# A hybrid decoder step: output projection and gate on token chunks of 448, 448 and 160, operands kept as whole rows

## The chip, the core and the metric

The kernel runs on one core of a Trainium2 chip. A core has a matrix engine (TensorE, "PE" in the profile, with its weight loads as "PEld"), a vector engine (DVE), a scalar engine (ACT), a general engine (POOL), a sync engine (SP) that here only issues transfers, and 16 DMA engines that serve all queues. Matmuls write to PSUM, in banks of 512 float32 columns; everything else lies in SBUF, 128 partitions wide. The metric is the device time of the whole program in microseconds, the median of several runs. Before the change it is 1441.19 us (3 runs, 1440.43 to 1441.89).

## The reference

One layer of a decoder for 1024 prompt tokens and 32 sample tokens (8 sequences of 4), 1056 tokens in all, width 1024. Cut to what the change touches, it ends so:

```python
y_a = o.reshape(B, T, V_W) @ w_proj_a                      # gated delta branch
y_b = (y_pool * silu(gp)) @ w_proj_b                       # pooling branch
m = sigmoid(ga) * y_a + sigmoid(gb) * y_b
x = x + m @ w_out                                          # output projection
x = x + sigmoid(rmsnorm(x, norm_ple) @ w_ple_gate) * (p_i @ w_ple_proj)   # per-layer gate
y = rmsnorm(x, final_norm)
```

What stands ahead of it (input projections, convolution, gated delta recurrence, pooling) is computed by the same program and is not changed but for one small edit named below.

## The kernel before

Everything is kept transposed: features on the partitions (8 tiles of 128), tokens along the free dimension. The 1056 tokens are cut into three chunks of 352 (`CW`, `NCH`). A dense product takes one weight tile (128 output features, all 1024 input features) and one chunk. For precision both operands are split into a high and a low part in a float32 form that the array takes in one pass (`F32R`), and `chunk` (L317) runs 8 times three matmuls: high weight by high data, high weight by low data, low weight by high data. So a product is 24 matmuls of 128x128 weights by 352 moving columns, each with a weight load of its own. Matmuls on plain float32 operands (the recurrence, the norms) appear in the trace as two records each.

The last part of the program, from L1554 on, has six passes. In the first three the output projection runs over the eight weight tiles for chunk 0, then chunk 1, then chunk 2; `ev_o` adds the residual from an addend that is loaded a step ahead into one of three buffers (`addend`), and ACT squares the result for the norm. When a pass is over, `norm_ple` is started: sums of squares by matmuls with one moving column, a Newton iteration on DVE (`rstd`, L407), a diagonal matrix `dg` whose product with ones spreads the factor over the partitions, and then per tile a scaling, a high part on ACT, a low part on DVE or POOL. The second three passes are the gate's product on chunk 0, 1, 2 (`ev_p`: tanh on ACT, two operations on DVE, square on ACT, sum on DVE), each followed by `norm_out`, which scales and stores the chunk. The very last tile is worked in two halves. Behind the last matmul stands the tail: that tile, the norm of the last chunk, eight scalings and eight stores.

The order of the work on each engine is written by a recording layer (`Weave`): generators such as `norm_ple` are advanced between matmuls whenever a planner's clock says that their inputs are due. The planner books a matmul of a product at 13 ns plus its columns over 2.4. The engines then run their own queues in order and wait on semaphores. The weights of the output projection are split once and stay (`resident`), loaded two tiles ahead during the first pass; those of the gate come in during the third pass. PSUM has four banks for the products (`psd`) here and two for the norms (`pse`).

Operands are tiles of 128 x 352, one for each feature tile and chunk (`set_tiles`, L301): `h` (normed input, later the pooled branch), `o` (delta branch), `m` (merged branch), and `g` (normed x for the gate) in the buffers of `m`.

Of the kernel before, what the change touches and what calls it, by code (L numbers as in the profile page):

```python
# [18 lines left out]
P = 128  # L19
D = 1024  # L20
KT = D // P
# [4 lines left out]
T = TP + TS  # L26
CW = 352
NCH = T // CW
H = 8
NU = TP // P  # L30
PH = 15
# [203 lines left out]
def decoder_step(ctx, tc, A, O):  # L235
    nc = tc.nc
    wv = Weave()
# [8 lines left out]
    def mm(o, l, r, ns, start=True, stop=True):  # L246
        PE.matmul(o, l, r, start=start, stop=stop)  # L247
        wv.pe(ns)
# [50 lines left out]
        eng.tensor_tensor(out=lo, in0=src, in1=hi.bitcast(F32), op=ALU.subtract)  # L299

    def set_tiles(p, name):  # L301
        mk = lambda s: [[p.tile([P, CW], F32R, name=f"{name}{s}{k}_{n}", tag=f"{s}{k}_{n}") for n in range(NCH)]
                        for k in range(KT)]
        return mk("h"), mk("l")

    def drained(g, ps, ring):

# [94 lines left out]
            if step:  # L402
                yield step

    RB = CW // 4

    def rstd(sqs, bank, mk, key=None, keys=()):  # L407


        ms, rs, tm = (mk([P, 4], nm)[0:RB] for nm in ("ms", "rs", "tm"))  # L410
        for j, parts in enumerate([sqs] if key else [[q] for q in sqs]):
            if j:
                yield keys
            pr = bank()[0:RB, 0:4]
            for j in range(4):
                for i, q in enumerate(parts):
                    mm(pr[:, j:j + 1], q[:, j * RB:(j + 1) * RB], ones[:, 0:1], 150, start=(i == 0),
                       stop=(i == len(parts) - 1))
# [8 lines left out]
        dg = mk([P, 4, RB], "dg")[0:RB]  # L427
        V.tensor_tensor(out=dg, in0=ident[0:RB, 0:RB].unsqueeze(1).broadcast_to([RB, 4, RB]),
                        in1=rs.unsqueeze(2).broadcast_to([RB, 4, RB]), op=ALU.mult)
        yield  # L430
        bc = bank()[:, 0:CW]
        mm(bc, ones[0:RB, :], dg.rearrange("p a b -> p (a b)"), 592)
        return bc


    hhi, hlo = set_tiles(sa, "h")
# [1033 lines left out]

# [36 lines left out]
    def heads_end():  # L1507
        hctx.close()
        so = octx.enter_context(pool("seto"))
        for l, t in zip((ohi, olo), set_tiles(so, "o")):  # L1510
            l.extend(t)
# [18 lines left out]
    psd = banks(ctx, "psd", PB)  # L1530


    mhi, mlo = set_tiles(sa, "m")
    with pool("ew", 2) as ew:
        for m in range(KT):
            ta = ew.tile([P, T], F32, name="ta2", tag="ta2")
# [16 lines left out]

    cq = ctx.enter_context(pool("outp", 2))  # L1554
    pse = ctx.enter_context(pool("pse", 2, space=PSUM))
    x1 = [[cq.tile([P, CW], F32, name=f"x1{k}_{n}", bufs=1) for n in range(NCH)] for k in range(KT)]
    ct = lambda nm, bufs=2: cq.tile([P, CW], F32, name=nm, tag=nm, bufs=bufs)

    def ssum(m, sqa, src, key):
        if m == 0 or m == KT - 1 and len(sqa) > 1:  # L1560
            S.activation(sqa[m > 0], src, AF.Square)
        else:
            q = ct("sq1")
# [5 lines left out]
    def rnorm(sqs, keys=()):  # L1569
        return rstd(sqs, lambda: pse.tile([P, 512], F32, name="pse", tag="pse"),  # L1570
                    lambda sh, nm: cq.tile(sh, F32, name=nm, tag=nm, bufs=1), keys=keys)

    ghi, glo = [[None] * NCH for _ in range(KT)], [[None] * NCH for _ in range(KT)]

    def norm_ple(n, sqa):
        yield [("o", 0, n, m) for m in range(KT)]
        yield
        rs = yield from rnorm(sqa)
        yield
        for k in range(KT):  # L1580
            hh = ct("hh")
            V.scalar_tensor_tensor(out=hh, in0=x1[k][n], scalar=nple[:, k:k + 1], in1=rs, op0=ALU.mult, op1=ALU.mult)
            yield
            ghi[k][n] = sa.tile([P, CW], F32R, name=f"gh{k}_{n}", tag=f"h{k}_{n}")
            glo[k][n] = sa.tile([P, CW], F32R, name=f"gl{k}_{n}", tag=f"l{k}_{n}")
            S.copy(ghi[k][n], hh)
            yield
            (G if k % 2 else V).tensor_tensor(out=glo[k][n], in0=hh, in1=ghi[k][n].bitcast(F32), op=ALU.subtract)
        wv.mark("ple", n)

    def norm_out(n, sqa):
        done = [("o", 1, n, m) for m in range(KT)]
        yield done[:-1] if len(sqa) > 1 else done
        yield
        rs = yield from rnorm(sqa, done)
        yield
        last = n == NCH - 1
        for k in range(KT):
            V.scalar_tensor_tensor(out=x1[k][n], in0=x1[k][n], scalar=nfin[:, k:k + 1], in1=rs,
                                   op0=ALU.mult, op1=ALU.mult)  # L1600
            SY.dma_start(O["yT"][k][:, ns_(n)], x1[k][n])
            if not last:
                yield

# [29 lines left out]

    adds = {}

    def addend(s):

        if s < 48:
            n, m = s % 24 // KT, s % KT  # L1640
            adds[s] = ct("xr2", 3)
            SY.dma_start(adds[s], (A["xT"] if s < 24 else pp_d)[m][:, ns_(n)])

    addend(0)
    for n in range(NCH):
        sqa = [ct("sqa")]
        for m in range(KT):
            s = n * KT + m
            weights_step(s)
            addend(s + 1)  # L1650

            def ev_o(n, c, o, xr=adds[s], m=m, sqa=sqa):
                V.scalar_tensor_tensor(out=x1[m][n], in0=o, scalar=0.5, in1=xr, op0=ALU.mult, op1=ALU.add)
                yield
                yield from ssum(m, sqa, x1[m][n], (0, n, m))
            chunk(held["w_out"][m], mhi, mlo, n, ev_o)
        wv.add(norm_ple(n, sqa))
    for n in range(NCH):
        wv.until(("ple", n), data=True)
        sqa = [ct("sqa")] + [ct("sqb")] * (n == NCH - 1)  # L1660
        for m in range(KT):
            s = 24 + n * KT + m
            weights_step(s)
            addend(s + 1)

            def ev_p(n, c, o, pq=adds[s], m=m, sqa=sqa):
                t, x = ct("tg"), x1[m][n]
                end = n == NCH - 1 and m == KT - 1
                w = CW // 2 if end else CW
                for a in range(0, CW, w):  # L1670
                    S.activation(t[:, a:a + w], o[:, a:a + w], AF.Tanh, scale=0.5)
                    if not end:
                        yield
                for a in range(0, CW, w):
                    V.scalar_tensor_tensor(out=pq[:, a:a + w], in0=t[:, a:a + w], scalar=1.0, in1=pq[:, a:a + w],
                                           op0=ALU.add, op1=ALU.mult)
                    V.tensor_tensor(out=x[:, a:a + w], in0=x[:, a:a + w], in1=pq[:, a:a + w], op=ALU.add)
                    if end:
                        S.activation(sqa[1][:, a:a + w], x[:, a:a + w], AF.Square)
                if end:  # L1680
                    wv.mark("o", 1, n, m)
                    return
                yield
                yield from ssum(m, sqa, x1[m][n], (1, n, m))
# [73 lines left out]
```

## Time and profile before

| what | value |
|---|---|
| median of 3 runs | 1441.19 us |
| the profiled execution | 1443.41 us |
| its span on the core | 1441.6 us |
| PE busy in the span | 1400.9 us (97%) |
| granted clock of TensorE, mean | 0.991 |
| the six passes | about 1233 to 1427 us of the span |
| behind the last matmul of a product | about 14.4 us |

The profile is of one execution, 2.2 us longer than the median, and its span leaves out 1.8 us around it. Shares of busy time are averages over stages. A matmul's duration in the trace (about 323 ns at 352 columns) contains its way through the array; the next one starts long before it ends, so the rate is read from starts, or from a count in a stretch without gaps.

### The profile page before, as it was taken

What the parts mean: (1) busy time and instruction counts of PE and PEld (TensorE: products, weight loads), DVE (VectorE), ACT (ScalarE), POOL (GpSimd) and SP (SyncE); (2) the same over time, 40 slices, a digit from 0 to 9 for tenths busy, and PEclk for the clock granted to TensorE, in tenths of its full rate; (3) what the DMA queues carried; (4) which work ended last, traced back from release to release, by engine and by line L of the source; (5) the groups of instructions that cost most, each with busy time, mean ns of one, the idle gap of its engine ahead of it and who ended that gap; (6) DMA issues with size and microseconds to landing.
All of it is one profiled execution on the core that took longest, in us unless ns stands there. A gap on an engine that the chain in (4) does not pass through costs nothing.

```text
span 1441.6 us, 24421 instructions
## 1 busy us (share of the span) xinstructions
PE 1400.9 (97%) x9138; PEld 1359.4 (94%) x9138; DVE 832.8 (58%) x1810; ACT 611.2 (42%) x1612; POOL 406.6 (28%) x336
## 2 busy tenths in 40 slices
PE   8899999999999999999999999999999999999996
PEld 7799999999999999999999899999889999999996
DVE  5686666665666635437457457457464244645654
ACT  5356565555454323544454454454223122324321
POOL 3444545454121222232132132032021112315100
PEclk9899999999999999999999999999999999999998
DMA  9222232223244413752234234236538434415132
GB/s 311 72 78 94 94 104 97 96 104 123 76 135 145 136 54 104 210 176 84 66 143 132 77 124 146 65 112 222 188 122 282 139 135 147 135 46 163 43 97 88
DMA packets 106235, 178.94 MB, mean 124 GB/s; under 512 B 19260, under 2 KB 78852, under 8 KB 106116
## 3 DMA queue, kind: packets, MB, share of 16 engines
q1 hardware_dynamic: 91716, 125.99, 26.7%
q10 hardware_dynamic: 14400, 51.39, 11.5%
q8 instruction: 72, 1.18, 0.3%
q14 instruction: 47, 0.39, 0.1%
HBM read 119.92 MB, written 57.41 MB: 123 GB/s over the span
## 4 chain that ended last, share of the span: by engine, by line
PE 84%; DVE 8%; DMA 4%; ACT 2%; issue 1%; SPq 1%; POOL 0%; ACTq 0%; DVEq 0%; POOLq 0%
PE psd L247 69%; PE psg L247 5%; PE psr L247 5%; PE psg L251 2%; DMA rw<-og_d 1%; PE sr L247 1%; DVE win L186 1%; DVE big L186 1%; DMA xt<-in_xT_dram 1%; PE sg L247 1%; PE pse L247 1%; DMA gt<-tb_d 1%; DMA pp_d<-ppt 1%; DVE sg L186 1%; DMA wr<-in_w_out_dram 1%
## 5 line engine op out<-in xcount | busy, mean ns | idle before, releaser
L247 PE MATMUL psd<-hh,wh 128*128 128x352 f32 x1728 | 570.1, 330 | 5.8 <-DVE gt L186 3.4
L247 PE MATMUL psd<-hh,wl 128*128 128x352 f32 x1728 | 567.2, 328 | 0.4 <-POOL wl L186 0.4
L247 PE MATMUL psd<-hl,wh 128*128 128x352 f32 x1728 | 565.9, 327 | 0.0
L186 POOL TENSOR_TENSOR wl<-wr,wh 128x1024 fp32r<-128x1024 f32 (+1 forms) x87 | 209.9, 2412 | 612.7 <-ACT wh L186 536.2
L247 PEld LDWEIGHTS psd<-hh,wh 128*128 128x128 f32 x1728 | 326.1, 189 | 9.4 <-DVE gt L186 4.3
L247 PEld LDWEIGHTS psd<-hl,wh 128*128 128x128 f32 x1728 | 326.4, 189 | 1.8 <-issue 0.3
L247 PEld LDWEIGHTS psd<-hh,wl 128*128 128x128 f32 x1728 | 326.0, 189 | 2.2 <-POOL wl L186 0.7
L186 DVE SCALAR_TENSOR_TENSOR acc<-xr,cw,acc 128x352 f32<-128x352 f32 x144 | 108.5, 772 | 37.3 <-ACT acc L186 35.9
L186 ACT CAST wh<-wr 128x1024 fp32r<-128x1024 f32 (+1 forms) x88 | 90.6, 1030 | 40.2 <-PE psd L247 26.7
L186 POOL TENSOR_TENSOR acc<-acc,f 128x352 f32<-128x352 f32 (+1 forms) x72 | 73.6, 1028 | 120.7 <-DVE acc L186 89.1
L186 DVE SCALAR_TENSOR_TENSOR f<-f,acc 128x352 f32<-128x352 f32 (+1 forms) x72 | 68.8, 956 | 48.2 <-ACT f L186 48.2
L186 ACT ACTIVATE gt<-psd 128x352 f32<-128x352 f32 x69 | 32.3, 468 | 113.4 <-PE psd L247 88.4
L186 DVE SCALAR_TENSOR_TENSOR gt<-gt,psd 128x352 f32<-128x352 f32 x48 | 24.8, 516 | 67.0 <-ACT gt L186 30.2
L247 PE MATMUL psd<-oh,wh 128*128 128x352 f32 x192 | 62.0, 323 | 0.7 <-DVE gt L186 0.7
L247 PE MATMUL psd<-oh,wl 128*128 128x352 f32 x192 | 61.6, 321 | 0.0
L247 PE MATMUL psd<-ol,wh 128*128 128x352 f32 x192 | 61.6, 321 | 0.0
L186 ACT COPY xr<-psd 128x352 f32<-128x352 f32 (+1 forms) x96 | 33.7, 377 | 61.1 <-PE psd L247 61.1
L186 ACT ACTIVATE f<-acc 128x352 f32<-128x352 f32 (+1 forms) x72 | 36.1, 502 | 53.0 <-POOL acc L186 41.3
L186 ACT ACTIVATE junk<-psg 128x128 f32<-128x128 f32 x128 | 36.2, 283 | 41.4 <-PE psg L251 39.7
L247 PE MATMUL psd<-mh,rl 128*128 128x352 f32 x144 | 46.5, 323 | 1.1 <-POOL rl L186 1.1
L247 PE MATMUL psd<-gh,rh 128*128 128x352 f32 x144 | 46.7, 325 | 0.0
L247 PE MATMUL psd<-mh,rh 128*128 128x352 f32 x144 | 46.5, 323 | 0.0
(289 smaller groups left out, 2521.1 us busy)
## 6 DMA issues: line engine op xcount, KB each, us to landing
wr<-in_w_in_dram ACTq DMA_DIRECT2D x64, 512.0 KB, 3.6
kq_d<-f SPq DMA_DIRECT2D x16, 512.0 KB, 2.6
F<-kq_d SPq DMA_DIRECT2D x16, 512.0 KB, 4.9
xt<-in_xT_dram SPq DMA_DIRECT2D x6, 704.0 KB, 7.4
pp_d<-ppt SPq DMA_DIRECT2D x24, 176.0 KB, 6.0
yh_d<-ysh SPq DMA_DIRECT2D x24, 176.0 KB, 2.0
yl_d<-ysl SPq DMA_DIRECT2D x24, 176.0 KB, 2.6
tb_d<-gt SPq DMA_DIRECT2D x24, 176.0 KB, 3.7
```

The costliest lines, as they stand in the source:

```text
L186: return f(*a, **k)
L247: PE.matmul(o, l, r, start=start, stop=stop)
L251: PE.transpose(o, i, idn)
```

## The change

The two products of the last part take chunks of 448, 448 and 160 tokens (`LAST`) in place of three of 352. The output projection goes over them in the order first, short, second; the gate in the order first, second, short, so that the short chunk is the last. The operand tiles `h`, `o` and `m` become whole rows of 1056 tokens that are cut into views (`cut`, `thirds`), and the normed x for the gate is written over `m` in place. `rstd` takes its width from the sums of squares. While the norm of the last chunk is computed, six matmuls without use (`keep`) run on TensorE. The loops over passes and tiles become one list of steps. Apart from that, in `both` (two pairs of weight tiles between the gates and the pooled branch's projection) the second weight's low part is computed by DVE, not by POOL.

```diff
+LAST = tuple(slice(a, b) for a, b in ((0, 448), (448, 896), (896, T)))
+LW = 448
...
     def set_tiles(p, name):
-        mk = lambda s: [[p.tile([P, CW], F32R, name=f"{name}{s}{k}_{n}", tag=f"{s}{k}_{n}") for n in range(NCH)]
-                        for k in range(KT)]
+        mk = lambda s: [p.tile([P, T], F32R, name=f"{name}{s}{k}", tag=f"{s}{k}") for k in range(KT)]
         return mk("h"), mk("l")
+
+    cut = lambda tiles, cols: [[t[:, c] for c in cols] for t in tiles]
+    thirds = lambda tiles: cut(tiles, [ns_(n) for n in range(NCH)])
...
-    def rstd(sqs, bank, mk, key=None, keys=()):
+    def rstd(sqs, bank, mk, key=None, keys=(), keep=0):
+        W = sqs[0].shape[1]
+        RB = W // 4
...
+        if keep:
+            idle = bank()
+            for _ in range(keep):
+                mm(idle[:, 0:P], ident, ident, 222)
...
                 if n == NCH - 1 and raws:
-                    wv.run(split_w())
+                    wv.run(split_w(G if w is ws[0] else V))
...
-    ghi, glo = [[None] * NCH for _ in range(KT)], [[None] * NCH for _ in range(KT)]
+    ghi, glo = mhi, mlo
...
-        rs = yield from rnorm(sqa, done)
-        yield
         last = n == NCH - 1
+        rs = yield from rnorm(sqa, done, 6 if last else 0)
+        yield
...
+    steps = [(j, n, m) for j, chunks in enumerate(((0, 2, 1), (0, 1, 2))) for n in chunks for m in range(KT)]
...
+        if j:
+            chunk(held["w_ple_gate"][m], ghi, glo, n, ev_p, cols=LAST[n])
+        else:
+            chunk(held["w_out"][m], mhi, mlo, n, ev_o, cols=LAST[n])
             if m == KT - 1:
-                wv.add(norm_out(n, sqa))
-            chunk(held["w_ple_gate"][m], ghi, glo, n, ev_p)
+                wv.add(norm_ple(n, sqa))
```

On PE, the second pass of the output projection (weights `wh`, `wl`, data `mh`, `ml`), around the sums of squares of the first chunk. Before:

```order
L247 MATMUL psd_10977<-mh_1_10982,wh 128x352
L247 MATMUL psd_10977<-ml_1_11006,wh 128x352
L247 MATMUL psd_10977<-mh_1_10982,wl 128x352
L247 MATMUL psd_10977<-mh_1_10985,wh 128x352
L247 MATMUL psd_10977<-ml_1_11009,wh 128x352
```

And now, at the same place:

```order
L249 MATMUL psd_10914<-mh_10917,wh 128x160
L249 MATMUL psd_10914<-ml_10925,wh 128x160
L249 MATMUL psd_10914<-mh_10917,wl 128x160
L249 MATMUL psd_10914<-mh_10918,wh 128x160
L249 MATMUL psd_10914<-ml_10926,wh 128x160
L249 MATMUL pse<-cst,sqa 112x1 x4
```

The sequence of weights is the same and so is the number of matmuls; the second pass is now the one on 160 columns, and the other two have 448.

On PE at the end of the program (`sqa`, `sqb` are the squares, `cst` the constants). Before:

```order
L247 MATMUL psd_10980<-gh_2_13036,rh_12805 128x352
L247 MATMUL pse<-cst,sqa 88x1 x4
L247 MATMUL psd_10980<-gl_2_13037,rh_12805 128x352
L247 MATMUL psd_10980<-gh_2_13036,rl_12806 128x352
L247 MATMUL psd_10980<-gh_2_13057,rh_12805 128x352
L247 MATMUL psd_10980<-gl_2_13058,rh_12805 128x352
L247 MATMUL psd_10980<-gh_2_13057,rl_12806 128x352
L247 MATMUL pse<-cst,sqb 88x1 x4
L247 MATMUL pse<-dg,cst 128x352
```

And now:

```order
L249 MATMUL psd_10916<-mh_10924,rh_12686 128x160
L249 MATMUL psd_10916<-ml_10932,rh_12686 128x160
L249 MATMUL psd_10916<-mh_10924,rl_12687 128x160
L249 MATMUL pse<-cst,sqa 40x1 x4
L249 MATMUL pse<-cst,sqb 40x1 x4
L249 MATMUL pse<-cst 128x128 x6
L249 MATMUL pse<-dg,cst 128x160
```

The first sums of squares moved behind the last matmul of the products, and the six matmuls of `keep` stand ahead of the one that spreads the factor.

On DVE, in the projection of the pooled branch (`os` are small operations of the recurrence's output norm, `gt` the evacuation of a product, `F` of the recurrence). Before:

```order
L186 TENSOR_TENSOR os_t_7283<-os_r_7282 128x8
L186 SCALAR_TENSOR_TENSOR os_t_7283<-os_t_7283,os_x_7281 128x8
L186 SCALAR_TENSOR_TENSOR os_r_7282<-os_t_7283,os_r_7282 128x8
L186 SCALAR_TENSOR_TENSOR gt_5767<-gt_5767,psd_5725 128x352
L186 SCALAR_TENSOR_TENSOR F_5746<-psg_5729,gn,F_5746 128x512
```

And now:

```order
L188 TENSOR_TENSOR os_t_7251<-os_r_7250 128x8
L188 SCALAR_TENSOR_TENSOR os_t_7251<-os_t_7251,os_x_7249 128x8
L188 SCALAR_TENSOR_TENSOR os_r_7250<-os_t_7251,os_r_7250 128x8
L188 TENSOR_TENSOR wl<-wr,wh 128x1024
L188 SCALAR_TENSOR_TENSOR gt_5735<-gt_5735,psd_5693 128x352
L188 SCALAR_TENSOR_TENSOR F_5714<-psg_5697,gn,F_5714 128x512
```

A split of 1024 columns (`wl`) that POOL did before stands on DVE, ahead of an evacuation; another stands some 60 us earlier.

## Rows read from the trace of the kernel before

**Rows 1.** The page's part 1: busy time, share of the span, instructions.

```profile
PE 1400.9 (97%) x9138; PEld 1359.4 (94%) x9138; DVE 832.8 (58%) x1810; ACT 611.2 (42%) x1612; POOL 406.6 (28%) x336
```

**Rows 2.** Stretches of the six passes: length; busy of PE, PEld, DVE, ACT, POOL; clock; DMA.

```profile
1233.00:1263.60 30.60, 29.51 (x184) 29.06 (x183) 19.70 (x18) 10.83 (x15) 11.97 (x5) 1.00 0.46 142
1263.60:1427.20 163.60, 163.28 (x1030) 160.61 (x1028) 93.37 (x211) 49.28 (x95) 31.67 (x20) 1.00 0.29 87
```

**Rows 3.** The same view, matmuls of the products alone, inside one pass.

```profile
1272.00:1299.00 27.00, 27.00 (x169) 27.00 (x168) 3.68 (x7) 0.00 (x0) 1.00 0.16 46
```

**Rows 4.** Float32 matmuls, 128 weight columns, 96 moving: by form, then in time.

```profile
L247 PE MATMUL psg<-U,U 128*128 128x96 f32 x128 | 16.6, 274 | 0.9 <-DVE U L186 0.9
...
683.24 1.03 PE L247 MATMUL psg<-U,U 128*128 128x96 f32 x8
...
688.97 1.06 PE L247 MATMUL psg<-U,U 128*128 128x96 f32 x8
```

**Rows 5.** PEld, then PE in time (start, length) as a product resumes.

```profile
602.57 0.19 PEld L247 LDWEIGHTS psd<-hh,wh 128*128 128x128 f32 x1
602.68 0.19 PEld L247 LDWEIGHTS psd<-hl,wh 128*128 128x128 f32 x1
602.85 0.19 PEld L247 LDWEIGHTS psd<-hh,wl 128*128 128x128 f32 x1
...
602.60 0.41 PE L247 MATMUL psd<-hh,wh 128*128 128x352 f32 x1
602.84 0.32 PE L247 MATMUL psd<-hl,wh 128*128 128x352 f32 x1
```

**Rows 6.** PE and POOL in time, in the first pass.

```profile
1244.87 0.32 PE L247 MATMUL psd<-ml,rh 128*128 128x352 f32 x1
1246.27 0.43 PE L247 MATMUL psd<-mh,rl 128*128 128x352 f32 x1 [1.09 <-POOL rl L186]
...
1243.84 2.38 POOL L186 TENSOR_TENSOR rl<-wr,rh 128x1024 fp32r<-128x1024 f32 x1 [16.83 <-ACT rh L186]
```

**Rows 7.** Engines in time, in the projection of the pooled branch.

```profile
1067.28 2.35 POOL L186 TENSOR_TENSOR wl<-wr,wh 128x1024 fp32r<-128x1024 f32 x1
...
1067.38 2.27 DVE L186 TENSOR_TENSOR os_t<-os_r 128x8 f32<-128x8 f32 x1
...
1069.68 0.17 DVE L186 SCALAR_TENSOR_TENSOR os_t<-os_t,os_x 128x8 f32<-128x8 f32 x1
...
1069.97 0.52 DVE L186 SCALAR_TENSOR_TENSOR gt<-gt,psd 128x352 f32<-128x352 f32 x1
...
1070.54 0.54 PE L247 MATMUL psd<-hh,wh 128*128 128x352 f32 x1 [2.74 <-DVE gt L186]
```

**Rows 8.** The tail: engines in time; last, a stretch as in rows 2.

```profile
1426.86 0.32 PE L247 MATMUL psd<-gh,rl 128*128 128x352 f32 x1
...
1432.31 0.52 DVE L186 TENSOR_TENSOR dg<-cst,rs 88x352 f32<-88x352 f32 x1
1432.98 1.51 PE L247 MATMUL pse<-dg,cst 88*128 88x352 f32 x2 [2.82 <-DVE dg L186]
1434.53 4.02 DVE L186 SCALAR_TENSOR_TENSOR x<-x,vec,pse 128x352 f32<-128x352 f32 x8 [1.70 <-PE pse L247]
1435.14 3.78 SPq L231 DMA_DIRECT2D out_yT_dram<-x  x8
...
1429.00:1430.00 1.00, 0.86 (x8) 0.77 (x7) 0.00 (x0) 0.35 (x1) 0.00 (x0) 0.55 0.00 0
```

**Rows 9.** Groups by form in the six passes: DVE at two widths.

```profile
L186 DVE SCALAR_TENSOR_TENSOR xr<-tg,xr 128x352 f32<-128x352 f32 x23 | 12.1, 525 | 22.0 <-ACT tg L186 22.0
...
L186 DVE SCALAR_TENSOR_TENSOR xr<-tg,xr 128x176 f32<-128x176 f32 x2 | 0.7, 338 | 1.2 <-ACT tg L186 1.2
```

**Rows 10.** SP's queue in time, issues one behind the other.

```profile
1008.08 0.42 SPq L231 DMA_DIRECT2D hl<-yl_d  x1
1008.60 0.38 SPq L231 DMA_DIRECT2D hh<-yh_d  x1
```

More of the change, by code (lines that the diff above doesn't have):

```diff
@@ L425, in rstd @@
                 V.scalar_tensor_tensor(out=ms, in0=pr, scalar=1.0 / D, in1=ms, op0=ALU.mult, op1=ALU.add)
+        if keep:
+            idle = bank()
+            for _ in range(keep):
+                mm(idle[:, 0:P], ident, ident, 222)
         yield from rsqrt_steps(rs, ms, tm, 0 if key else 100)
-        dg = mk([P, 4, RB], "dg")[0:RB]
-        V.tensor_tensor(out=dg, in0=ident[0:RB, 0:RB].unsqueeze(1).broadcast_to([RB, 4, RB]),
+        dg = mk([P, CW if key else LW], "dg")[0:RB, 0:W]
+        V.tensor_tensor(out=dg.rearrange("p (a b) -> p a b", a=4), in0=ident[0:RB, 0:RB].unsqueeze(1).broadcast_to([RB, 4, RB]),
                         in1=rs.unsqueeze(2).broadcast_to([RB, 4, RB]), op=ALU.mult)
         yield
-        bc = bank()[:, 0:CW]
-        mm(bc, ones[0:RB, :], dg.rearrange("p a b -> p (a b)"), 592)
+        bc = bank()[:, 0:W]
+        mm(bc, ones[0:RB, :], dg, 1.68 * W)
         return bc
-    hhi, hlo = set_tiles(sa, "h")
+    hhi, hlo = map(thirds, set_tiles(sa, "h"))
     sq = kp.tile([P, 3, H * TS], F32, name="sq")
@@ L1510, in heads_end @@
         for l, t in zip((ohi, olo), set_tiles(so, "o")):
-            l.extend(t)
+            l.extend(thirds(t))
         op = octx.enter_context(pool("rwp"))
@@ L1530, in decoder_step @@
     psd = banks(ctx, "psd", PB)
-    mhi, mlo = set_tiles(sa, "m")
+    mset = set_tiles(sa, "m")
+    mhi, mlo = map(thirds, mset)
     with pool("ew", 2) as ew:
@@ L1555, in decoder_step @@
     pse = ctx.enter_context(pool("pse", 2, space=PSUM))
-    x1 = [[cq.tile([P, CW], F32, name=f"x1{k}_{n}", bufs=1) for n in range(NCH)] for k in range(KT)]
-    ct = lambda nm, bufs=2: cq.tile([P, CW], F32, name=nm, tag=nm, bufs=bufs)
+    width = [c.stop - c.start for c in LAST]
+    mhi, mlo = (cut(t, LAST) for t in mset)
+    x1 = [[cq.tile([P, w], F32, name=f"x1{k}_{n}", bufs=1) for n, w in enumerate(width)] for k in range(KT)]
+    ct = lambda nm, n, bufs=2: cq.tile([P, LW], F32, name=nm, tag=nm, bufs=bufs)[:, 0:width[n]]
     def ssum(m, sqa, src, key):
@@ L1562, in ssum @@
         else:
-            q = ct("sq1")
+            q = ct("sq1", key[1])
             S.activation(q, src, AF.Square)
@@ L1567, in ssum, with rnorm @@
         wv.mark("o", *key)
-    def rnorm(sqs, keys=()):
+    def rnorm(sqs, keys=(), keep=0):
         return rstd(sqs, lambda: pse.tile([P, 512], F32, name="pse", tag="pse"),
-                    lambda sh, nm: cq.tile(sh, F32, name=nm, tag=nm, bufs=1), keys=keys)
-    ghi, glo = [[None] * NCH for _ in range(KT)], [[None] * NCH for _ in range(KT)]
+                    lambda sh, nm: cq.tile(sh, F32, name=nm, tag=nm, bufs=1), keys=keys, keep=keep)
+    ghi, glo = mhi, mlo
     def norm_ple(n, sqa):
@@ L1580, in norm_ple @@
         for k in range(KT):
-            hh = ct("hh")
+            hh = ct("hh", n)
             V.scalar_tensor_tensor(out=hh, in0=x1[k][n], scalar=nple[:, k:k + 1], in1=rs, op0=ALU.mult, op1=ALU.mult)
             yield
-            ghi[k][n] = sa.tile([P, CW], F32R, name=f"gh{k}_{n}", tag=f"h{k}_{n}")
-            glo[k][n] = sa.tile([P, CW], F32R, name=f"gl{k}_{n}", tag=f"l{k}_{n}")
             S.copy(ghi[k][n], hh)
@@ L1594, in norm_out @@
         yield
-        rs = yield from rnorm(sqa, done)
+        last = n == NCH - 1
+        rs = yield from rnorm(sqa, done, 6 if last else 0)
         yield
-        last = n == NCH - 1
         for k in range(KT):
@@ L1600, in norm_out @@
                                    op0=ALU.mult, op1=ALU.mult)
-            SY.dma_start(O["yT"][k][:, ns_(n)], x1[k][n])
+            SY.dma_start(O["yT"][k][:, LAST[n]], x1[k][n])
             if not last:
@@ L1635, in decoder_step @@
     adds = {}
+    steps = [(j, n, m) for j, chunks in enumerate(((0, 2, 1), (0, 1, 2))) for n in chunks for m in range(KT)]
     def addend(s):
[L1639 to L1642, printed above, removed]
+        if s < len(steps):
+            j, n, m = steps[s]
+            adds[s] = ct("xr2", n, 3)
+            SY.dma_start(adds[s], (pp_d if j else A["xT"])[m][:, LAST[n]])
     addend(0)
[L1645 to L1653, printed above, removed]
-                yield
-                yield from ssum(m, sqa, x1[m][n], (0, n, m))
-            chunk(held["w_out"][m], mhi, mlo, n, ev_o)
-        wv.add(norm_ple(n, sqa))
@@ L1658, in decoder_step @@
[L1658 to L1679, printed above, removed]
-                if end:
[L1681 to L1684, printed above, removed]
@@ new lines, in decoder_step, with ev_o, ev_p @@
+    for s, (j, n, m) in enumerate(steps):
+        last = j and n == NCH - 1
+        if m == 0:
+            if j:
+                wv.until(("ple", n), data=True)
+            sqa = [ct("sqa", n)] + [ct("sqb", n)] * last
+        weights_step(s)
+        addend(s + 1)
+        def ev_o(n, c, o, xr=adds[s], m=m, sqa=sqa):
+            V.scalar_tensor_tensor(out=x1[m][n], in0=o, scalar=0.5, in1=xr, op0=ALU.mult, op1=ALU.add)
+            yield
+            yield from ssum(m, sqa, x1[m][n], (0, n, m))
+        def ev_p(n, c, o, pq=adds[s], m=m, sqa=sqa):
+            t, x, cw = ct("tg", n), x1[m][n], width[n]
+            end = n == NCH - 1 and m == KT - 1
+            w = cw // 2 if end else cw
+            for a in range(0, cw, w):
+                S.activation(t[:, a:a + w], o[:, a:a + w], AF.Tanh, scale=0.5)
+                if not end:
+                    yield
+            for a in range(0, cw, w):
+                V.scalar_tensor_tensor(out=pq[:, a:a + w], in0=t[:, a:a + w], scalar=1.0, in1=pq[:, a:a + w],
+                                       op0=ALU.add, op1=ALU.mult)
+                V.tensor_tensor(out=x[:, a:a + w], in0=x[:, a:a + w], in1=pq[:, a:a + w], op=ALU.add)
+                if end:
+                    S.activation(sqa[1][:, a:a + w], x[:, a:a + w], AF.Square)
+            if end:
+                wv.mark("o", 1, n, m)
+                return
+            yield
+            yield from ssum(m, sqa, x1[m][n], (1, n, m))
+        if j and m == KT - 1:
+            wv.add(norm_out(n, sqa))
+        if j:
+            chunk(held["w_ple_gate"][m], ghi, glo, n, ev_p, cols=LAST[n])
+        else:
+            chunk(held["w_out"][m], mhi, mlo, n, ev_o, cols=LAST[n])
```

1 line of the change is left out of this document (removed).

## The prediction

> **What bounds the kernel now.** First comes the page's busy table: PE is busy 97% of the span, and every one of its 9138 matmuls has a weight load of its own [rows 1]. Next, the view by stretches over the six passes that are re-cut: PE is busy 163.28 of 163.60 us after the first pass, at a clock of 1.00, while DVE has 93 us of work there and ACT 49 [rows 2]. So in these passes time is the number of matmuls times the distance between their starts, and the other engines matter only in the first pass, where PE misses 1.1 us, and in the tail. The distance is read from a stretch without gaps: 169 matmuls in 27.00 us, 159.8 ns at 352 columns [rows 3]. At the clock's upper level of 2.4 GHz 352 columns stream in 146.7 ns, so 13.1 ns of it are something else.
>
> Then I looked for the least distance that a load of 128 weight columns allows, since the change makes matmuls shorter and not fewer. Two views show it. In the recurrence, float32 matmuls with 128 weight columns move 96 columns in two passes over the data (80 ns at 2.4 GHz), yet eight of them stand (1.03 - 0.274)/7 = 108 ns apart, and eight others (1.06 - 0.274)/7 = 112 ns [rows 4]. That is float32; for the one-pass form of the products the timeline shows it where a product resumes after a short interruption: its first two weight loads start 602.57 and 602.68, 0.11 us apart, though later ones keep to the matmuls' 0.16 [rows 5]. The second load can start when the array has taken the first, so a load takes about 108 ns there too. At 352 columns it hides behind the stream; at 160 columns it can't.
>
> **The change, part by part.** *Matmuls.* The passes keep 6 x 8 x 24 = 1152 matmuls and their columns: 768 at 448 columns, 384 at 160. If distance were linear in width, nothing would change, because 2 x 448 + 160 = 3 x 352. No row shows a one-pass matmul narrower than 352, so the linear value at 160 has two readings: 66.7 + 13.1 = 79.8 ns if the 13.1 ns are fixed, 159.8 x 160/352 = 72.6 ns if they go with the columns. The load holds the real distance at 108 to 112 ns [rows 4, 5]; I take 110 ns, the middle. The surplus is 30 to 37 ns, I take 34.4, and over 384 matmuls 13.2 us. From below it is 108 - 79.8 = 28 ns, 10.8 us. From above, if the 13.1 ns come on top of the load, 121 ns against 72.6, 18.6 us. All of it lies on PE, which nothing covers.
>
> The Trainium skill (TensorE: Matmul & The Clock Gate, Back-to-back issue gap) speaks against this: it gives a sustained 81 ns for a pair of load and matmul at 128 columns and 131 ns at 512. By that, 160 columns would go at about 84 ns and the passes would lose 2 to 4 us, an estimate from that page. The rows speak for the other side: 159.8 ns at 352 columns is already above the page's figure for 512 [rows 3], and 108 ns at 96 columns above its figure for 128 [rows 4].
>
> *First pass.* In the fourth weight tile of the first pass PE waits from 1244.87 to 1246.27 for the low part that POOL computes from 1243.84 on [rows 6]. With 448 columns a tile takes 24 x 203 ns = 4.9 us, not 3.8, so the fourth begins about 3 us later, near 1247.7, while load, cast and split of the weight keep their times and end at 1246.2. The gap of 1.40 us shrinks to a step of 0.16: -1.25 us. If ACT's queue moves the load by as much as the matmuls, the gain is nothing.
>
> *The tail.* It runs from the last matmul's start at 1426.86 to 1441.6. DVE costs (525 - 338)/176 = 1.06 ns a column [rows 9], so a row operation on 160 columns takes 0.32 us, not 0.52. The last tile's four half operations lose 0.1 us each, but the order now puts one scaling of the chunk before, 448 wide (0.63 us), behind them, ahead of the operation that reads the last sums; both together gain 0.1. `dg` gains 0.2. The matmul that spreads the factor took 1.51 us, at a clock that had fallen to half after the products ended (0.55 between 1429 and 1430) [rows 8]; at 160 columns its stream is 160/352 of that, and with 0.2 us of latency I put it at 0.8, gain 0.7, whether or not the six extra matmuls raise the clock; if they do, 1.0. They follow the last sums and end before `dg` is ready 2.6 us later. The eight scalings go 0.50 us apart, DVE's pace [rows 8]; at 0.32 SP's pace takes over, 0.5 us an issue [rows 10], so only the first result comes earlier: 0.2. The last store is 80 KB in place of 176; 0.3. Sum -1.5 us; bounds 0 (should DVE in the last pass fall behind) and -3.
>
> DVE has room in the short passes: a tile there takes PE 24 x 110 = 2.64 us, 21 us for a pass, against three operations of 0.32 a tile and the norm of a 448 chunk, eight scalings of 0.63 and some 3 us of small ones, together about 16 us. The addends are issued a step ahead into three buffers, as before.
>
> *DVE for POOL.* In the pooled branch's projection POOL's split of 2.35 us and a 128x8 operation of DVE run together, and DVE's takes 2.27, where the next of its size needs 0.17; the evacuation behind it comes at 1069.97 and PE waits 2.74 us for its bank [rows 7]. The order shows this split on DVE now, later than that evacuation: the 2.1 us are no longer in its way, and the split (1.2 us on DVE, an estimate from half of POOL's time) stands ahead of the next one, for which PE has a chunk of 3.8 us in hand. That gives back up to 1.9 us. The other split moved to DVE stands in the inversion of the last heads, where PE waits for DVE, and may cost 0.6. I take -1.3; bounds -2.2 and +0.8.
>
> *Whole rows.* Contents and addresses within a row are the same, and in the order every matmul that waits names the same kinds of producers; I cost it at nothing. What hides it is that chunk 0 of the gate runs 39 us while the second chunk is normed; without that cover it is a rival below.
>
> Sum: 13.2 - 1.25 - 1.5 - 1.3 = +9.15 us. The profiled execution of 1443.41 us would become 1452.6. It lay 2.2 us above the median; on 1441.19 the sum gives **1450.3 us**.
>
> **The rivals.**
> A. Forecast: the weight load sets 110 ns. With the bounds of the small terms it runs from 1445.5 to 1455. For it: both views of the load. Against it: no narrow one-pass matmul in the trace. Chance 0.75.
> B. The 13.1 ns are a cost of each matmul behind its load, not of its columns: 121 ns, surplus 41 to 48 ns, about 17 us, so 1454 to 1456. For it: the stretch at 352 is 13.1 above the stream [rows 3]. Against it: the float32 matmuls show 0 to 4 ns above the load [rows 4]. Chance 0.13.
> C. Faster: the array takes weights ahead fast enough in the one-pass form that distance stays linear; surplus 0 and the small gains stand: 1441.2 - 4.05 = 1437.1. It decides from below 80 ns at 160 columns. For it: PE runs ahead with loads in the stretch at 352. Against it: the 0.11 us between two such loads [rows 5], which no amount of running ahead shortens when every matmul has its own. Chance 0.04.
> D. In between, loads at some 84 ns, the distance of the page quoted above: surplus 4 to 11 ns, 2 to 4 us, cancelled by the gains: 1439 to 1442. For it only that the loads of the products were never pressed. Chance 0.03.
> E. Whole rows make a wait coarser: a gate matmul on chunk 0 waits for the norm of the second chunk, since both lie in one tile. Then PE stands for that norm, about 0.9 us of DVE a tile and 3 us of small operations, some 10 us, once: 1460. Against it: waits as named in the order. Chance 0.04.
> F. The clock falls in the short passes, where the array streams 67 of 110 ns: at 1.2 GHz a load takes 216 ns, surplus 140 ns in 384 matmuls, 54 us, 1495. Against it: it fell only where PE stood idle [rows 8]. Chance 0.01.
>
> **How the numbers follow.** Two in ten left out: the range goes from 1445.5, the low end of A, to 1456, which takes in B. Less than 0.2% (2.9 us, 1438.3 to 1444.1) can't be told from no change here. Faster is C with a little of D: 0.05. Same is D with the lowest end of A: 0.05. Slower is the rest, 0.90.
>
> **What would show it.** In the profile after, a stretch inside the short passes has about 24 matmuls in 2.64 us, with PEld as busy as can be, and a short pass lasts 21 us plus its norm; at 79 ns it would be 15 us and C holds, at 121 ns 23 us and B. The two long passes of a product go at about 200 to 204 ns a matmul, which tells whether the 13.1 ns are fixed. The gap in the first pass should be gone; the evacuation after the split should no longer hold PE for 2.7 us; the tail from the last product matmul should be 13.3 us and not 14.8; the clock should stay 1.00 until the last product. The prediction is wrong if the short passes are not limited by the loads, or if new waits of PE appear between passes.

## The result: slower by 0.6%, and where it lies in the profile after

The changed kernel takes 1449.59 us (median of 6 runs, 1448.19 to 1451.67) against 1441.43 us (6 runs) for the kernel before: a ratio of 1.0059, 95% interval 1.0045 to 1.0072. The forecast was 1450.3 with a range of 1445.5 to 1456. The profiled execution took 1448.19 us, its span is 1446.3. One execution of the kernel without the six extra matmuls (below), 1995.56 us at a mean clock of 0.648 and without a profile, is left out of its median and ratio.

First the page's busy table of the changed kernel, which answers to [rows 1]:

```profile
PE 1414.1 (98%) x9150; PEld 1363.1 (94%) x9150; DVE 821.0 (57%) x1812; ACT 611.5 (42%) x1612; POOL 402.3 (28%) x334
```

PE is busy 13.2 us more and DVE 11.8 us less, though the columns that the products move are the same. Next the view by stretches, one row for each pass and one for the tail, cut at the first matmul of each pass and at the last one of a product (length; busy of PE, PEld, DVE, ACT, POOL; clock; DMA share and rate):

```profile
1226.58:1265.42 38.84, 38.84 (x195) 36.08 (x193) 12.84 (x18) 11.42 (x15) 12.00 (x5) 1.00 0.38 118
1265.42:1288.36 22.94, 22.94 (x203) 22.57 (x202) 11.47 (x34) 5.74 (x13) 2.30 (x2) 1.00 0.15 42
1288.36:1329.55 41.19, 40.16 (x205) 36.63 (x205) 19.84 (x44) 14.81 (x26) 21.47 (x13) 1.00 0.48 148
1329.55:1369.96 40.41, 40.41 (x203) 37.24 (x202) 22.61 (x46) 13.48 (x24) 7.18 (x6) 1.00 0.15 46
1369.96:1410.80 40.84, 40.71 (x204) 37.09 (x203) 21.37 (x43) 8.99 (x16) 0.00 (x0) 1.00 0.26 83
1410.80:1433.63 22.83, 22.83 (x203) 22.46 (x201) 14.11 (x42) 5.39 (x16) 0.00 (x0) 1.00 0.25 84
1433.63:1446.30 12.67, 4.43 (x33) 3.60 (x31) 5.97 (x26) 0.90 (x4) 0.00 (x0) 0.62 0.27 89
```

In the two short passes (second and sixth row) the weight loads fill 98% of the stretch, in the long ones 89 to 93%. That share alone doesn't tell what limits a pass: at 352 columns it was 98% too [rows 2]. The distance between starts does. The clock is 1.00 in all six passes.

The distance is read as in [rows 3], matmuls of the products alone in stretches without gaps; the first row lies in a short pass, the second in long ones:

```profile
1276.00:1288.00 12.00, 12.00 (x110) 12.00 (x109) 1.30 (x4) 0.00 (x0) 1.00 0.18 52
1303.00:1330.00 27.00, 27.00 (x136) 25.07 (x135) 3.38 (x6) 0.00 (x0) 1.00 0.50 160
```

12.00 us by 110 is 109 ns at 160 columns, 27.00 by 136 is 199 ns at 448 (a matmul cut by an edge counts too; the medians of the distances between neighbouring starts are 111 and 202 ns, and 160 to 161 before). The timeline of a short pass shows them one by one, three loads first, then three matmuls, each 0.11 us behind the last:

```profile
1423.84 0.19 PEld L249 LDWEIGHTS psd<-mh,rl 128*128 128x128 f32 x1
1423.95 0.19 PEld L249 LDWEIGHTS psd<-mh,rh 128*128 128x128 f32 x1
1424.06 0.19 PEld L249 LDWEIGHTS psd<-ml,rh 128*128 128x128 f32 x1
...
1423.80 0.28 PE L249 MATMUL psd<-ml,rh 128*128 128x160 f32 x1
1423.91 0.28 PE L249 MATMUL psd<-mh,rl 128*128 128x160 f32 x1
1424.02 0.28 PE L249 MATMUL psd<-mh,rh 128*128 128x160 f32 x1
```

To say where time went, each trace is cut at the starts of four matmuls: the last step of the recurrence, the first matmul of the delta branch's projection, the first of the six passes, and the last of a product. The first column begins with the span, the last one (the tail) ends with it. All values are of one profiled execution, in us.

| profiled execution | up to the recurrence's end | rest of the pooled projection | delta projection | six passes | tail |
|---|---|---|---|---|---|
| before | 1059.6 | 81.67 | 91.81 | 193.75 | 14.76 |
| after | 1058.3 | 76.65 | 91.65 | 207.05 | 12.69 |
| after, a second profile | 1059.6 | 77.49 | 91.82 | 207.04 | 13.16 |
| equal chunks, rest changed | 1059.2 | 78.58 | 91.82 | 192.69 | 14.49 |
| before, with the split on DVE | 1057.1 | 77.11 | 91.82 | 193.65 | 14.48 |
| 400, 400, 256 | 1059.3 | 76.72 | 91.65 | 194.37 | 13.19 |
| 160 with half loads | 1061.1 | 76.72 | 91.82 | 193.92 | 12.82 |

The passes lose 13.3 us, in both profiles of the changed kernel alike; the rest of the pooled projection gains 4 to 5, the tail 1.6 to 2.1. The first column scatters by 4 us from execution to execution. Most of that is chance and not the change: at 1008 us, ahead of the first of the two moved splits, the traces are already 3 us apart. That is why a term of one microsecond is better read from its own stretch than from the whole time.

### The profile page after: what moved, and what is told of

Read it like the earlier page. It is cut to its first block, busy times and chain, and to the rows that moved or that the text cites. A ratio compares the mean times of both kernels' runs of the same rounds, so it can differ in the third digit from the quotient of the medians.

```text
span 1446.3 us, 24439 instructions
## 1 busy us (share of the span) xinstructions
PE 1414.1 (98%) x9150; PEld 1363.1 (94%) x9150; DVE 821.0 (57%) x1812; ACT 611.5 (42%) x1612; POOL 402.3 (28%) x334
## 4 chain that ended last, share of the span: by engine, by line
PE 87%; DVE 7%; ACT 2%; DMA 2%; issue 1%; SPq 0%; ACTq 0%; POOL 0%; DVEq 0%
PE psd L249 73%; PE psr L249 5%; PE psg L249 5%; PE psg L253 2%; PE sr L249 1%; DVE win L188 1%; DVE big L188 1%; PE pse L249 1%; PE sg L249 1%; DMA xt<-in_xT_dram 1%; DVE sg L188 1%; DMA pp_d<-ppt 1%; DVE sqs L188 1%; SPq L233 0%; ACT junk L188 0%
## 5 line engine op out<-in xcount | busy, mean ns | idle before, releaser
L188 POOL TENSOR_TENSOR wl<-wr,wh 128x1024 fp32r<-128x1024 f32 (+1 forms) x85 | 205.3, 2416 | 591.5 <-ACT wh L188 485.1
L249 PE MATMUL psd<-ml,rh 128*128 128x448 f32 (+1 forms) x288 | 96.9, 336 | 0.0
L249 PE MATMUL psd<-mh,rh 128*128 128x448 f32 (+1 forms) x288 | 96.9, 336 | 0.0
L249 PE MATMUL psd<-mh,rl 128*128 128x448 f32 (+1 forms) x288 | 96.5, 335 | 0.0
L249 PEld LDWEIGHTS psd<-ml,rh 128*128 128x128 f32 x288 | 54.5, 189 | 3.3 <-issue 0.6
```

What stands on the lines that cost most here:

```text
L188: return f(*a, **k)
```

## The experiments

**Equal chunks.** The widths alone are undone:

```diff
-LAST = tuple(slice(a, b) for a, b in ((0, 448), (448, 896), (896, T)))
+LAST = tuple(slice(a, b) for a, b in ((0, 352), (352, 704), (704, T)))
```

> The changed kernel with chunks of 352, 352 and 352; whole rows, the order of the passes, the six extra matmuls and the split on DVE stay. Theory (the loss is the weight load at 160 columns and nothing else): the matmuls of the passes go 160 ns apart as before, the stall of 1.4 us in the first pass is back, the split's gain of the trace (PE was 4.9 us further at the start of the delta branch's projection, beyond what it was ahead before) stays: 1435 to 1438 us. Rival 1 (whole rows make waits coarser and cost part of it): over 1441. Rival 2 (the 4.9 us were chance of one execution, the split gives the 1.3 that were forecast): 1439.5 to 1441.

Measured: 1438.15 us, 0.9973 times before (0.9963 to 0.9983), just above the 1435 to 1438 of the theory and below both rivals. The passes take 192.69 us, 14.4 less than with 160. So the loss hangs on the widths. Whole rows cost nothing that can be seen: the next run, which keeps the old tiles, has the same time within its interval. One part of the expectation missed: the stall of the first pass did not come back.

**The split alone.** The kernel before with one line of the change:

```diff
-                    wv.run(split_w())
+                    wv.run(split_w(G if w is ws[0] else V))
```

> The kernel before with nothing changed but the second weight's low part in the two pairs of the pooled branch computed by DVE. Theory: it gives what the two traces show up to the start of the delta branch's projection, 3.5 to 5 us: 1436.5 to 1438, the wait of 3.07 us shrinks to about 1 and the two later ones of 0.45 and 0.93 go. Rival (as forecast): 1.3 us, 1440. Rival (chance): 1441.4.

Measured: 1437.79 us, 0.9965 (0.9953 to 0.9978). By the ratio that is a gain of 5.1 us with an interval of 3.2 to 6.8 (the medians are 4.4 apart); the forecast's 1.3 lies outside. At the place where PE stood for 1.40 us in the first pass the distance is 0.31 us here, without a change of widths.

**A last chunk of 256.**

```diff
-LAST = tuple(slice(a, b) for a, b in ((0, 448), (448, 896), (896, T)))
+LAST = tuple(slice(a, b) for a, b in ((0, 400), (400, 800), (800, T)))
```

> The changed kernel with chunks of 400, 400 and 256. Theory (distance is the larger of 110 ns for the load and 0.454 ns a column): 256 columns go at 116 ns, so there is no surplus; with the split's gain and a tail some 1.5 us shorter than before 1434.5 to 1438. Rival 1 (13.1 ns go on top of the stream wherever the matmul is short): 120 to 123 ns, 1.5 to 2.7 us more, 1437 to 1440. Rival 2 (each short pass loses by its own norm and not by its loads): about as slow as 160, 1447 and above.

Measured: 1437.28 us, 0.9967 (0.9955 to 0.9978). A stretch of a short pass at 256 columns, matmuls of the products:

```profile
1272.00:1282.00 10.00, 10.00 (x88) 10.00 (x87) 1.70 (x4) 0.00 (x0) 1.00 0.17 47
```

10.00 by 88 is 114 ns, with the cut ones in the count; the median is 118 (0.46 ns a column), where the theory had 116 and rival 1 had 120 to 123, and the time lies in the range of both. So this run doesn't tell these two apart; the half loads below do. What it shows is that the surplus is nearly gone: the six passes take 194.37 us, 1.7 more than equal chunks and 12.7 less than with 160.

**A last chunk of 128**, for its time and then once more for its profile:

```diff
-LAST = tuple(slice(a, b) for a, b in ((0, 448), (448, 896), (896, T)))
+LAST = tuple(slice(a, b) for a, b in ((0, 464), (464, 928), (928, T)))
```

> The changed kernel with chunks of 464, 464 and 128. Theory (the load is a floor): 110 ns again at 128 columns, where 0.454 ns a column would be 58; the surplus over 384 matmuls is 20.0 us in place of 14.4 at 160, so 5 to 6 us above the changed kernel: 1454 to 1456. Rival (a short matmul pays a fixed 37 ns on top of its columns): 95 ns, the same surplus as at 160, 1449 to 1450.

Measured: the profiled execution has a median distance of 111 ns at 128 columns, passes of 212.43 us and 1455.57 us in all, as the floor demands; a fixed 37 ns a matmul, which would give 95, falls. But only two of six executions took 1455 us. Two took 1472 at a mean clock of 0.98, two 1484 and 1488 at 0.97.

> The kernel with chunks of 464, 464 and 128 once more, for its profile: its executions took 1455, 1472 and 1484 to 1488 us, with mean clocks of 0.993, 0.982 and 0.970 to 0.973, and the profile is of one at 1455.6. Theory (in some executions TensorE's clock falls to 1.2 GHz in one short pass or in both): a profile of 1470 or more shows a clock near 0.5 in a short pass, with distances near 220 ns, and no wait. Rival (the lost time is a wait, and the clock falls in it): a gap of PE of 16 us or several that make it up. If this execution also takes 1455 us, nothing is told apart.

Measured: 1483.89 us at a mean clock of 0.972. First stretches of its two short passes, all engines (the first row begins in the long pass ahead), then the matmuls at the place where the clock begins to fall:

```profile
1264.00:1272.00 8.00, 8.00 (x54) 7.48 (x53) 2.23 (x5) 1.42 (x3) 0.00 (x0) 1.00 0.07 16
1272.00:1282.00 10.00, 10.00 (x71) 10.00 (x70) 3.40 (x17) 0.69 (x3) 0.00 (x0) 0.74 0.09 20
1282.00:1300.00 18.00, 18.00 (x81) 17.13 (x80) 3.84 (x10) 2.67 (x6) 1.17 (x1) 0.50 0.08 21
...
1446.00:1468.40 22.40, 22.40 (x101) 21.53 (x101) 6.68 (x17) 2.24 (x8) 0.00 (x0) 0.50 0.19 70
```

```profile
1276.51 0.27 PE L249 MATMUL psd<-ml,rh 128*128 128x128 f32 x1
1276.62 0.28 PE L249 MATMUL psd<-mh,rl 128*128 128x128 f32 x1
1276.74 0.30 PE L249 MATMUL psd<-mh,rh 128*128 128x128 f32 x1
1276.85 0.41 PE L249 MATMUL psd<-ml,rh 128*128 128x128 f32 x1
1277.06 0.42 PE L249 MATMUL psd<-mh,rl 128*128 128x128 f32 x1
1277.27 0.41 PE L249 MATMUL psd<-mh,rh 128*128 128x128 f32 x1
```

The clock falls to 0.50, that is 1.2 GHz, in the middle of a pass with PE busy and no wait of PE ahead of it, and the distance goes from 0.11 to 0.21 us. It stays there until wide matmuls come again: between 1305 and 1400 us it is 0.99. This is rival F, at 128 columns.

**Half loads.** In the short passes 64 weight columns are loaded instead of 128, so this kernel leaves out the lower 64 rows of each result there:

```diff
+        q = 64 if cols.stop - cols.start == 160 else P
...
-            c = slice(k * P, (k + 1) * P)
+            c = slice(k * P, k * P + q)
...
-            mm(o, whi[:, c], xhi[k][n], ns, start=(k == 0), stop=False)
+            mm(o[0:q], whi[:, c], xhi[k][n], ns, start=(k == 0), stop=False)
...
```

> The changed kernel, but the matmuls of the two short passes load 64 weight columns in place of 128: the lower 64 rows of their result are not computed, everything behind them works on what lies in the bank. Theory (the load sets 110 ns): in the trace before, float32 matmuls with 64 weight columns and 64 moving ones stand 55 to 58 ns apart, so such a load no longer limits and 160 columns go at 73 to 80 ns; 384 matmuls gain 30 to 37 ns each: 11.5 to 14 us below the changed kernel, 1435.5 to 1438, unless DVE, with some 16 us of work a short pass, becomes the limit of a pass of 14 to 15 us, which would take 1 to 2 us a pass of it back. Rival (a one-pass matmul with 160 moving columns needs 110 ns of its own, whatever its weights): 1449 to 1450.

Measured: 1437.19 us, 0.9976 (0.9964 to 0.9988), against 1.0059 for the full loads: 12 us less. Three neighbours in its short pass:

```profile
1276.08 0.24 PE L249 MATMUL psd<-mh,rl 128*64 128x160 f32 x1
1276.15 0.24 PE L249 MATMUL psd<-mh,rh 128*64 128x160 f32 x1
1276.23 0.24 PE L249 MATMUL psd<-ml,rh 128*64 128x160 f32 x1
```

The median is 73 ns, the linear value of the prediction, with the same moving data and the same number of instructions. So 160 moving columns don't need 110 ns; 128 weight columns do. The edit halves the rows of the result along with the load, and this run alone doesn't tell those two apart. That it is the load rests on [rows 5], where two loads start 0.11 us apart with no narrow matmul between them.

**A new wait.** The changed kernel stands once in its second long pass. PE, DVE and POOL in time there:

```profile
1298.88 0.37 PE L249 MATMUL psd<-ml,rh 128*128 128x448 f32 x1
1300.28 0.51 PE L249 MATMUL pse<-dg,cst 40*128 40x160 f32 x2 [1.03 <-DVE dg L188]
...
1297.67 2.47 DVE L188 TENSOR_TENSOR dg<-cst,rs 40x160 f32<-40x160 f32 x1
...
1297.58 2.38 POOL L188 TENSOR_TENSOR wl<-wr,wh 128x1024 fp32r<-128x1024 f32 x1
```

The small `dg` takes DVE as long as POOL's split beside it. The edit gives that split to DVE:

```diff
-        split(raw, whi, wlo, V if (name, m) == ("w_out", 2) else G)
+        split(raw, whi, wlo, V if (name, m) in (("w_out", 2), ("w_ple_gate", 0)) else G)
```

> The changed kernel with the low part of the first weight tile of the gate computed by DVE, not by POOL. In the changed kernel's trace PE stands 1.40 us in the second pass on 448 columns, waiting for the diagonal matrix of the short chunk's norm, an operation of 160 columns that takes DVE 2.47 us while POOL works on that split. Theory (DVE is held by POOL's split): the operation takes 0.3 us, the wait goes, and nothing else moves: 1.0 to 1.3 us less, 1448.3 to 1448.6. Rival (the operation is slow or late by itself, or the split of 1.2 us on DVE holds up the next evacuation): no gain, or up to 1 us more.

Measured: 1447.40 us, 1.0050 (1.0034 to 1.0065). The same operation now, and its matmul without a wait:

```profile
1297.22 0.32 DVE L188 TENSOR_TENSOR dg<-cst,rs 40x160 f32<-40x160 f32 x1
```

```profile
1298.73 0.54 PE L249 MATMUL pse<-dg,cst 40*128 40x160 f32 x2
```

The passes go from 207.05 to 205.97 us: the wait cost 1.08. The whole time agrees, but its interval alone would not have shown it. In the traces with chunks of 464 and 128 or of 400 and 256 this wait doesn't occur, so it hangs on when the two operations fall.

**Without the six extra matmuls.**

```diff
-        rs = yield from rnorm(sqa, done, 6 if last else 0)
+        rs = yield from rnorm(sqa, done, 0)
```

> The changed kernel without the six extra matmuls in the tail. Theory (they hold the clock up): the matmul that spreads the factor runs at 1.2 GHz and takes 0.2 to 0.4 us longer, the rest of the tail stays: 1449.8 to 1450. Rival (they are in the way): up to 0.5 us shorter. A time alone may not tell so little; the trace of the tail does, by the distance of the two records of that matmul, 0.40 us with the extra matmuls.

Measured: 1453.76 us, 1.0088 (1.0070 to 1.0105), from three executions, neither theory nor rival. Its trace puts the difference ahead of the passes (first column 1061.3 us, the six passes 207.06), so it was run again beside the changed kernel on one chip.

> The changed kernel without the six extra matmuls once more. Its median was 4 us above the changed kernel's, but its trace shows the tail only 0.23 us longer (12.91 against 12.68 us behind the start of the last product matmul), and PE 4.4 us later already at the start of the delta branch's projection. Theory (the 4 us are chance of the stages ahead, which are the same in both): beside the control on the same chip it is 0 to 0.5 us slower. Rival (without the matmuls something ahead runs later, though the order of its instructions is the same): again 3 us or more.

> The changed kernel itself, as a control on the same chip as the two others of this call, since medians of the kernel before differed by 2 us between chips: 1.0045 to 1.0072 times the kernel before.

Measured: 1450.63 us, 1.0069 (1.0056 to 1.0082), beside 1448.93, 1.0054 (1.0040 to 1.0068) for the changed kernel. The intervals overlap, and the tails (12.75 us without the extra matmuls, 13.16 with them) go against the order of the times. The matmul that spreads the factor, without the extra ones, and then in the changed kernel:

```profile
1440.45 0.87 PE L249 MATMUL pse<-dg,cst 40*128 40x160 f32 x2 [2.58 <-DVE dg L188]
```

```profile
1436.32 2.53 PE L249 MATMUL pse<-cst 128*128 128x128 f32 x12
...
1438.96 0.87 PE L249 MATMUL pse<-dg,cst 40*128 40x160 f32 x2
```

The stretch of that matmul, as in the view by stretches:

```profile
1438.90:1439.60 0.70, 0.64 (x2) 0.50 (x2) 0.00 (x0) 0.00 (x0) 0.00 (x0) 0.50 0.00 0
```

In this execution they didn't hold the clock: 0.50, and 0.87 us either way. In the execution with the gate's split on DVE the same matmul took 0.51. And in the second profile of the changed kernel they were in the way:

```profile
1438.82 2.93 PE L249 MATMUL pse<-cst 128*128 128x128 f32 x12
...
1441.00 0.32 DVE L188 TENSOR_TENSOR dg<-cst,rs 40x160 f32<-40x160 f32 x1
...
1441.67 0.90 PE L249 MATMUL pse<-dg,cst 40*128 40x160 f32 x2
```

Here the matmul starts 0.35 us behind the end of `dg`, against 0.15 without the extra ones. Whether they gain anything on the average stays open; in the profiled tails it is at most some tenths, either way.

**Chunks of 400, 400 and 256, and both splits of the two pairs on DVE.** On top of the run with 256 one line changes:

```diff
-                    wv.run(split_w(G if w is ws[0] else V))
+                    wv.run(split_w(V))
```

> Chunks of 400, 400 and 256, and in the two pairs of weight tiles both splits on DVE, not only the second. In the trace at 256 PE waits 0.78 us for a low part that POOL starts late and then 0.95 us for an evacuation behind small DVE operations held by POOL. Theory (POOL's split holds DVE, so DVE's own is shorter for both): the first of the two waits goes, 0.5 to 1 us less than at 256 with one split: 0.9950 to 0.9965 times the kernel before. Rival (the split that now stands in the inversion of the last heads, where PE waits for DVE, takes 1.2 us of it back): the same as at 256, 0.9955 to 0.9978, or up to 1 us more.

Measured: 1434.77 us, 0.9955 (0.9943 to 0.9968), the fastest of all. In its trace the two waits are gone, and the rest of the pooled projection takes 75.04 us. Against 256 with one split the intervals overlap; against both kernels of this case they don't. No part of that gain is shown to come from the chunks: passes and tail together take 207.16 us here (194.38 and 12.78) and 207.18 with equal chunks. Equal chunks with both splits on DVE were not run.

## Why the prediction was right, and where a step was not

**Matmuls, +13.2: right.** The long passes go at 202 ns (200 to 204 were forecast), the short ones at 111 (110). The six passes grew by 13.30 us. The surplus itself is the difference to equal chunks, 14.36 us, less the new wait of 1.08: 13.28. Half loads show the cause, 128 and 256 columns the two sides of the floor. The reading of [rows 4] could have been sharper: the 108 ns has in it one first distance of 82 ns, and the other thirteen are 111 to 112. Rival B (121 ns) and rival C (below 80) fall with the distance, and so does rival D (84).

Rival D went by the Trainium skill (TensorE: Matmul & The Clock Gate, Back-to-back issue gap), which gives 81 ns at 128 columns; the matmuls of this kernel have 111 there. The Trainium skill (TensorE: Matmul & The Clock Gate, LDWEIGHTS) has a load take its weight columns over 1.2 GHz; for 128 that is an estimate of 107 ns, and the 111 at 128 and at 160 columns come within 4 ns of it.

**DVE for POOL, -1.3 with bounds of -2.2 and +0.8: wrong in size.** This is the step that failed. The rest of the pooled projection gained 5.0 us (4.2 in the second profile), and the split alone 5.1 in time. "The evacuation after the split should no longer hold PE for 2.7 us" came true. In the kernel before, the last matmul ahead of the wait in [rows 7] is this one:

```profile
1067.47 0.32 PE L247 MATMUL psd<-hh,wl 128*128 128x352 f32 x1
```

The same two matmuls in the changed kernel:

```profile
1066.13 0.32 PE L249 MATMUL psd<-hh,wl 128*128 128x352 f32 x1
...
1067.10 0.43 PE L249 MATMUL psd<-hh,wh 128*128 128x352 f32 x1 [0.64 <-DVE gt L188]
```

Between these starts lie 0.97 us, where 3.07 lay before: 2.1 us, about the 1.9 that the prediction allowed. Two things had been left out. First, the clock fell in the long wait, and the matmuls behind it went slower. These are two stretches behind it in the kernel before, and then one at the same place in the changed kernel, where the clock stays 1.00:

```profile
1070.50:1073.50 3.00, 2.96 (x12) 2.90 (x13) 1.39 (x8) 0.00 (x0) 1.86 (x2) 0.53 0.80 233
1073.50:1076.00 2.50, 2.50 (x17) 2.48 (x17) 1.30 (x2) 0.00 (x0) 0.18 (x1) 0.88 0.35 103
...
1067.10:1070.00 2.90, 2.90 (x19) 2.88 (x20) 2.73 (x9) 0.00 (x0) 1.79 (x1) 1.00 0.20 67
```

At 0.53 and 0.88 of the clock, 5.5 us of matmuls lose some 3.00 x 0.47 + 2.50 x 0.12 = 1.7 us, an estimate. Counted from the recurrence's end, the same matmul starts 2.1 us earlier than before right behind the wait, and 3.5 us earlier some 150 product matmuls on, in each of the eleven traces with this one split moved (3.50 to 3.54). So the steady gain is 3.5 us, and 1.4 of it arose behind the wait, near that estimate.

Second, in the kernel before DVE was held once more, by a later split, which the change leaves on POOL:

```profile
1108.40 2.40 POOL L186 TENSOR_TENSOR wl<-wr,wh 128x1024 fp32r<-128x1024 f32 x1 [5.97 <-ACT wh L186]
...
1108.54 2.64 DVE L186 TENSOR_TENSOR ol<-rw,oh 128x352 fp32r<-128x352 f32 x1
...
1113.38 0.43 PE L247 MATMUL psd<-hh,wh 128*128 128x352 f32 x1 [0.61 <-DVE gt L186]
```

There it left distances of 0.45 and 0.93 us on PE, where 0.16 is usual. With the change all of this comes earlier, and how the later operations fall differs from trace to trace: from there to the projection's end the eleven traces lose up to 0.4 us or gain up to 1.5, which makes 3.1 to 5.0 us in all. The 0.6 us that the prediction put down for the other moved split isn't seen: from 1008 us to the recurrence's end the same traces differ from the kernel before by -1.1 to +0.2 us.

**New waits of PE: not in the sum.** The short chunk's norm now meets POOL's split of the gate's first weights, 1.08 us, as shown above. The prediction named new waits of PE between passes as a sign of being wrong. This one stands inside a pass, at the norm of the chunk before, and counts as such a sign, though a small one. The prediction had seen DVE held by POOL's split in one place and didn't ask where else the new order brings the two together. The Trainium skill (SBUF — State Buffer, SBUF: two separate sides) says that a vector operation with two SBUF inputs and a GpSimd operation that reads SBUF exclude each other for a whole instruction. The rows agree: DVE operations took 2.27, 2.47 and 2.64 us beside splits of 2.35, 2.38 and 2.40 us that had started just ahead of them, and `dg` took 0.32 without one.

**First pass, -1.25: the gap is gone, but not by the widths alone.** The pass has no distance of starts in it above 0.21 us. But the gap is gone with equal chunks too, and down to 0.31 us with the split alone. What differs is one load of weights, 512 KB, on which the low part of that fourth tile waited; its time from issue to landing, before and then with the split alone:

```profile
wr<-in_w_out_dram ACTq DMA_DIRECT2D x1, 512.0 KB, 4.5
...
wr<-in_w_out_dram ACTq DMA_DIRECT2D x1, 512.0 KB, 3.5
```

With equal chunks it took 3.4 us, in the changed kernel 3.6. The low part was ready 13.1 us into the pass before, and 11.9 to 12.1 us in these three. So the 1.40 us belong to one profiled execution, and no run shows that the kernel before usually has them. Chunks of 448 do give slack: PE comes to that tile 14.6 us into the pass, in place of 11.6.

**Tail, -1.5: right.** 12.69 us, and 13.16 in the second execution, against 14.76; 13.3 were forecast. The rows that answer to [rows 8]:

```profile
1438.50 0.32 DVE L188 TENSOR_TENSOR dg<-cst,rs 40x160 f32<-40x160 f32 x1
...
1439.87 2.42 DVE L188 SCALAR_TENSOR_TENSOR x<-x,vec,pse 128x160 f32<-128x160 f32 x8 [1.05 <-PE pse L249]
1440.27 3.66 SPq L233 DMA_DIRECT2D out_yT_dram<-x  x8
```

`dg` gains 0.20 (0.2), its matmul 0.64 (0.7). The scalings now go 0.30 us apart, and SP's eight issues take 3.66 us, so SP sets the pace, as said. That the six extra matmuls end before `dg` is ready did not hold in the second profile, as shown above.

**Whole rows, 0: right**, by the equal chunks; rival E did not occur. **Rival F** did not occur at 160 columns, where all eleven executions of the changed kernel show a mean clock of 0.993 to 0.995; at 128 it did.

So the total was hit closer than its terms deserve, and that part is luck: a gain 2.9 to 3.7 us larger than forecast stands beside a wait of 1.1 that was not in the sum, and beside the scatter of the stages ahead. Without the first column the two profiles of the changed kernel give +6.0 and +7.5 us against the profile before; the sum said 9.15, and the medians say 8.2.

## What to carry to other kernels

When a product's matmuls are cut narrower and their number stays, compare the stream with the weight load first: here 0.46 ns a moving column against 110 ns, so below some 240 columns (an estimate from these two) each matmul pays for its load and nothing hides it. A short last chunk belongs at that width and not under it. Even there it is not sure to pay: at 256 the tail was 1.3 us shorter than with equal chunks and the passes 1.7 us longer, and the times don't tell the two apart. And when a split or an elementwise operation on POOL runs at the time of small DVE operations on the critical path, count DVE as blocked for all of POOL's time, and look at the clock behind the wait too: here that was 1.4 us more, behind a wait of 2.7.

## What the runs showed of the hardware that was not expected

The 13.1 ns above the stream at 352 columns are for the most part no fixed cost: the medians are 73 ns at 160 (half loads), 118 at 256, 160 at 352, 182 at 400 and 202 at 448, that is 0.45 to 0.46 ns a column throughout, where 2.4 GHz gives 0.417. A straight line through them leaves some 3 ns fixed, an estimate.

TensorE's clock can fall with PE busy all the time: at 128 columns, one every 111 ns, five of seven executions took 16 to 33 us longer at a mean clock of 0.970 to 0.982, and the one of them with a profile shows the fall from 1.00 to 0.50; at 160 none of eleven did. What decides it in an execution is not shown. So the penalty of narrow matmuls can have a second step, and a single run of such a kernel may miss it.
